# Order of the triangular solve of quarters two to four, and the PSUM bank of its combination

## The chip, the cores and the metric

The kernel runs on one core of a Trainium2 chip. The metric is the device time of one execution in microseconds, as the median of several runs of the same program. The core has a matrix engine (TensorE, PE in the profile; its weight loads are PEld), a vector engine (VectorE, DVE), an activation engine (ScalarE, ACT), a general engine (GpSimd, POOL) and a queue engine from which most DMAs are issued (SyncE, SP). Each engine works through its own list of instructions in the order in which the program has them, and waits on semaphores for the others.

## The reference

One inference step of a one-layer decoder trunk, over 512 prompt tokens and 8 x 8 sampled tokens (576 columns in the kernel). A shared projection feeds two groups of heads: a state-space group (SSD) and an RWKV-7 group, whose recurrence is

```python
def step(s, inp):
    r_t, w_t, k_t, v_t, kk_t, a_t = inp
    s_kk = jnp.einsum('bhvk,bhk->bhv', s, kk_t)
    s = (s * w_t[:, :, None, :] - s_kk[..., None] * (kk_t * a_t)[:, :, None, :]
         + v_t[..., None] * k_t[:, :, None, :])
    return s, jnp.einsum('bhvk,bhk->bhv', s, r_t)
```

with `kk = k*k_k / max(norm(k*k_k), 1e-12)` per head. Its readout goes through a norm per head, a bonus term and an output gate. Both groups then go through one output projection, a gated feed-forward layer, a per-layer embedding gate and a final norm. The step returns the two outputs and the new states.

## The kernel before

Activations lie transposed, 128 channels by 576 tokens. A projection is a sum of three matmuls per block, since weights and activations are split into a high and a low part (`whi`, `wlo`, `xhi`, `xlo`; L221 to L223 and L234). Weights come in blocks of 512 columns (`raw`, three buffers); ScalarE makes the high part (L93), GpSimd and VectorE in turn the low part (L206).

The RWKV heads are worked in four quarters (`Q[0]` to `Q[3]`; `s.q` is 0 for the first) of four heads each, two channel tiles `jj` with two heads `e`. In tokens there are nine groups `g` of 64: the sampled tokens and eight stretches of the prompt. A quarter goes through these steps:

- `fill_for` runs the six projections that the quarter needs; `fill` runs further projections of the list `todo` (the convolved columns `xbc`, the `z` gate) wherever the program puts them.
- `prep` makes the key norms and the decays. The sums of squared keys (L496) go to the PSUM bank `cb`, of which there is one (`cb_ps`); the square root of ScalarE (L93) that follows frees it. The transposes of the norms (`by_channel`, L523 and L526) use `cb` too.
- `start_states` (L734) multiplies the stored sampled states, loaded into `S0` (L723), also into `cb`. `S0` shares one buffer, tag `L`, with the matrix of the substitution and with the `S0` of `sampled` (L846 to L854).
- `gram` forms the products within a group (L613) and leaves a strictly triangular matrix per group and head in `Lst` (L623). `bonus` (L246, L598) and `decayed` (L650) follow.
- `inverse` is `solve` and then `combine`. `solve` needs the inverse of each 64 x 64 unit triangular matrix. It cuts the two diagonal blocks of 32 x 32 out through HBM (`Ld`, `L`), so that 72 blocks lie on 72 partitions, and inverts them on VectorE by substitution: 30 steps of two small instructions, each of which needs the one before (L674, L676). The results go through HBM back (`Td`, `Ad`), by SyncE's queue. `combine` loads them (`TT`, `AA`, L688 and L690), and makes the block below the diagonal with two small products: `Wp` (64 matmuls, L698), its eviction with a change of sign (L705 on VectorE, L93 on ScalarE), and `Xp` (64 matmuls, L712) with its eviction into `TT` (L719, L93). Both products took a bank of `cx_ps`, of which there are two.
- `chain` walks the nine groups in sequence (`core`, `prompt_state`, `outp`, `sampled`), with all its products in `cx` banks (L789, L797, L802, L812, L823, L849), and with small evictions on VectorE (L792, L805, L831) and ScalarE.
- `head_norm` is the norm per head of the quarter's result, with four products (L901) and the transposes of its norms (L523, L526) in `cx` banks.

The last quarter's `inverse`, `chain` and `head_norm` stand further down, among the start of the SSD part (`ssd`, a generator whose parts are called up by `SEQ`). There two kinds of fill are tied to a place: `issue_after(marks[...])` puts a `z` projection behind the last product (L901) of the third quarter's head norm (`("n", 2)`), the next one behind the last product L698 of the fourth quarter's combination (`("c", 3)`), and others behind steps of the fourth chain. The banks `r`, `y` and `d` of the SSD part open when the head norm of the last quarter is through.

The order on each engine is made when the program is built. A planner goes through a model of time; whenever an engine is free it gives it, out of the instructions that are ready in the model, the one that is first in the priority list, and it hands out buffers and banks on the way. The list is the order in which the code is written. `tc.high_priority()` puts the instructions of a block at the top of that list; the kernel has it at one place, the head norm of the last quarter. On the chip each engine then keeps that order.

Of the kernel before, what the change touches and what calls it, by code (L numbers as in the profile page):

```python
# [75 lines left out]
def hybrid_step(ctx, tc, A):  # L76
# [11 lines left out]
    def nm(s):  # L88
        uid[0] += 1
        return f"{s}_{uid[0]}"  # L90

    def act(out, in_, func=AF.Copy, scale=1.0, bias=0.0):
        return S.activation(out, in_, func, bias=bias, scale=scale)  # L93
# [16 lines left out]
    def bank(pool, tag, bufs):  # L110
        return pool.tile([P, 512], F32, tag=tag, name=nm(tag), bufs=bufs)
# [154 lines left out]
    def cx_ps():  # L266
        return bank(sq_, "cx", 2)
# [216 lines left out]
    def fill_at(s, i):  # L484
        fill(FP[s.q][i])
# [166 lines left out]
    def solve(s):  # L652

        q = s.q
        Ld = dp.tile([2, 2, 18, 32, 32], F32, tag=f"Ld{q}", name=f"Ld{q}")
        s.Td = dp.tile([2, 2, 18, 32, 32], F32, tag=f"Td{q}", name=f"Td{q}")
        s.Ad = dp.tile([2, 18, 32, 32], F32, tag=f"Ad{q}", name=f"Ad{q}")
        NB = 72
        for z in range(2):
            for e in range(2):  # L660
                r0 = e * 64 + z * 32
                nc.sync.dma_start(Ld[z, e].rearrange("g s t -> s g t"),
                                  s.Lst[r0:r0 + 32, :, :, z * 32:z * 32 + 32].rearrange("s g j t -> s (g j) t"))
        L = sp.tile([NB, 32, 32], F32, tag="L", name=nm("L"))
        nc.sync.dma_start(L[:], Ld[:].rearrange("z e g s t -> (z e g) s t"))
        Tt = s2.tile([NB, 32, 32], F32, tag="Tt", name=nm("Tt"))
        V.tensor_scalar(Tt[:], L[:], -1.0, None, ALU.mult)
        V.tensor_tensor(Tt[:].rearrange("p s t -> p (s t)")[:, 0:1024:33],
                        Tt[:].rearrange("p s t -> p (s t)")[:, 0:1024:33], ones[0:NB, 0:32], ALU.add)
        tmp = s2.tile([NB, 256], F32, tag="tmp", name=nm("tmp"))  # L670
        for jx in range(1, 31):
            n = 31 - jx
            o = tmp[:, 0:jx * n].rearrange("p (s t) -> p s t", s=jx)
            V.tensor_tensor(o, L[:, jx:jx + 1, jx + 1:32].to_broadcast([NB, jx, n]),  # L674
                            Tt[:, 0:jx, jx:jx + 1].to_broadcast([NB, jx, n]), ALU.mult)
            V.tensor_tensor(Tt[:, 0:jx, jx + 1:32], Tt[:, 0:jx, jx + 1:32], o, ALU.subtract)  # L676
        V.tensor_copy(L[0:36], Tt[0:36].rearrange("p s t -> p t s"))
        nc.sync.dma_start(s.Td[:].rearrange("z e g s t -> (z e g) s t"), Tt[:])
        nc.sync.dma_start(s.Ad[:].rearrange("e g s t -> (e g) s t"), L[0:36])

    def combine(s):

        TT = s.TT = inverses[s.q % 2]
        AA = s2.tile([P, 9, 2, 32], F32, tag="AA", name=nm("AA"))
        for e in range(2):
            for z in range(2):
                r0 = e * 64 + z * 32
                nc.sync.dma_start(TT[r0:r0 + 32, :, :, z * 32:z * 32 + 32].rearrange("s g j t -> s (g j) t"),  # L688
                                  s.Td[z, e].rearrange("g s t -> s g t"))
            nc.sync.dma_start(AA[e * 64:e * 64 + 32].rearrange("s g j t -> s (g j) t"),  # L690
                              s.Ad[e].rearrange("g s t -> s g t"))
        Wp = cx_ps()
        Wv = Wp[:].rearrange("p (g j t) -> p g j t", g=8, j=2)
        for g in range(1, 9):
            for jj in jj2:
                for e in range(2):
                    lo_, hi_ = e * 64, e * 64 + 32
                    marks["c", s.q] = T.matmul(Wv[hi_:hi_ + 32, g - 1, jj, :], s.Lst[lo_:lo_ + 32, g, jj, 32:64],  # L698
                                               AA[lo_:lo_ + 32, g, jj, :], start=True, stop=True)
        for e in range(2):  # L700
            hi_ = e * 64 + 32
            if e:
                act(AA[hi_:hi_ + 32, 1:9], Wv[hi_:hi_ + 32], scale=-1.0)
            else:
                V.tensor_scalar(AA[hi_:hi_ + 32, 1:9], Wv[hi_:hi_ + 32], -1.0, None, ALU.mult)  # L705
        Xp = cx_ps()
        Xv = Xp[:].rearrange("p (g j t) -> p g j t", g=8, j=2)
        for g in range(1, 9):
            for jj in jj2:
                for e in range(2):  # L710
                    lo_, hi_ = e * 64, e * 64 + 32
                    T.matmul(Xv[lo_:lo_ + 32, g - 1, jj, :], AA[hi_:hi_ + 32, g, jj, :],  # L712
                             TT[hi_:hi_ + 32, g, jj, 32:64], start=True, stop=True)
        for e in range(2):
            lo_ = e * 64
            if e:
                act(TT[lo_:lo_ + 32, 1:9, :, 32:64], Xv[lo_:lo_ + 32])
            else:
                V.tensor_copy(TT[lo_:lo_ + 32, 1:9, :, 32:64], Xv[lo_:lo_ + 32])  # L719
# [199 lines left out]
                YR.append(split(y, xp, ("xhi", "xlo"), [P, NT], lo_eng=V))  # L919

    def inverse(s):
        solve(s)
        fill_at(s, 7)
        combine(s)

    for s in Q:
        if s.q == 0:
            fill(2)
            gates(ugh)
        fill_for(s)  # L930
        prep(s)
        start_states(s)
        gram(s)
        bonus(s)
        decayed(s)
        if s.q < 3:
            inverse(s)
            chain(s)
            head_norm(s)
# [307 lines left out]
    steps = ssd()  # L1247
    next(steps)
    inverse(Q[3])
    s2_.close()  # L1250
    late.append(mix2.enter_context(tc.tile_pool(name="mf", bufs=1, reuse_waits="tile")))
# [421 lines left out]
```

## Time and profile before

| | us |
|---|---|
| median of three runs | 1342.29 |
| lowest and highest | 1341.25, 1345.83 |
| span of the profiled execution | 1349.0 |

The profile shows no other time of that execution than its span, from the first to the last instruction. All positions below are microseconds from its start. The profile is read with the engines' busy times, tables of windows, timelines of an engine (start, duration, engine, line, operation, what it writes and reads; in brackets the idle time before it and what ended it), groups of instructions by line, and lists of waits. A busy TensorE is not one at full speed: the granted clock is given beside it, 1.00 being full.

The chain of work that ended last is mostly TensorE's:

```profile
PE 63%; DVE 14%; ACT 4%; issue 4%; DMA 3%; POOL 3%; DVEq 0%; SPq 0%; ACTq 0%; POOLq 0%
```

The four quarters lie one after the other in the first half of the span: their substitutions start at 146.7, 276.2, 418.4 and 536.5 us. The chain of a quarter overlaps with the projections, the preparation and the substitution of the next one.

### The profile page before, as it was taken

Reading aid. Unit: us, or ns where it says so; the run is one execution under the profiler, and the core shown is the slowest. Engines: PE = TensorE matmul, PEld = TensorE weight load, DVE = VectorE, ACT = ScalarE, POOL = GpSimd, SP = SyncE. Lnnn points to the kernel's source line nnn. Section 1 sums busy time; section 2 is a strip of 40 time slices with the busy share of each in tenths; the row PEclk is TensorE's granted clock in tenths of the full one; section 3 lists DMA queues with packets and bytes.
Section 4 is the critical chain, followed back from the end, with each engine's and each line's share of the span. In section 5 each row is a group of like instructions: output and inputs, shape, how many; then the busy total and the mean of one; then the engine's idle time right before and its main releaser. Section 6 shows DMA issues by size and latency. Waiting matters only on the chain.

```text
span 1349.0 us, 26596 instructions
## 1 busy us (share of the span) xinstructions
PE 1246.8 (92%) x10525; PEld 1150.7 (85%) x10525; DVE 826.0 (61%) x1443; ACT 618.9 (46%) x1256; POOL 625.6 (46%) x597
## 2 busy tenths in 40 slices
PE   6897999999989978899999969989999999999997
PEld 6787897889868957788779859889999999999997
DVE  6648666887687785943466667886553135443454
ACT  6565436534654463343434364464442124433363
POOL 5425413642355154122456645565654336654642
PEclk9897799899979978889989989998999999999998
DMA  5322242234232412262454542222323222314322
GB/s 164 125 68 66 77 117 63 85 103 116 75 99 78 109 41 80 94 214 83 157 176 131 179 125 72 73 93 88 92 88 87 79 86 82 93 59 149 96 89 71
DMA packets 94461, 135.58 MB, mean 100 GB/s; under 512 B 34705, under 2 KB 39057, under 8 KB 94337
## 3 DMA queue, kind: packets, MB, share of 16 engines
q1 hardware_dynamic: 93760, 133.36, 32.4%
q8 instruction: 83, 1.36, 0.4%
q10 hardware_dynamic: 576, 0.52, 0.1%
q14 instruction: 42, 0.34, 0.1%
HBM read 106.10 MB, written 27.75 MB: 99 GB/s over the span
## 4 chain that ended last, share of the span: by engine, by line
PE 63%; DVE 14%; ACT 4%; issue 4%; DMA 3%; POOL 3%; DVEq 0%; SPq 0%; ACTq 0%; POOLq 0%
PE lin L234 21%; PE lin L1403 8%; PE lin L223 6%; PE lin L221 6%; PE lin L222 6%; DVE h L395 2%; PE lin L1508 1%; PE lin L1509 1%; PE lin L1510 1%; DVE tmp L674 1%; DVE wlo L206 1%; DVE Tt L676 1%; PE lin L613 1%; PE cx L797 1%; DVE suv L831 1%
## 5 line engine op out<-in xcount | busy, mean ns | idle before, releaser
L206 POOL TENSOR_TENSOR wlo<-raw,whi 128x512 fp32r<-128x512 f32 (+1 forms) x108 | 146.4, 1356 | 352.5 <-ACT whi L93 269.5
L93 ACT ACTIVATE whi<-raw 128x512 fp32r<-128x512 f32 (+1 forms) x232 | 143.3, 618 | 259.1 <-PE lin L234 126.4
L221 PE MATMUL lin<-xhi,whi 128*128 128x288 f32 (+1 forms) x784 | 243.3, 311 | 2.5 <-ACT whi L93 2.2
L223 PE MATMUL lin<-xhi,wlo 128*128 128x288 f32 (+1 forms) x784 | 241.5, 308 | 2.3 <-POOL wlo L206 2.3
L222 PE MATMUL lin<-xlo,whi 128*128 128x288 f32 (+1 forms) x784 | 241.5, 308 | 0.3 <-POOL xlo L194 0.3
L206 DVE TENSOR_TENSOR wlo<-raw,whi 128x512 fp32r<-128x512 f32 (+1 forms) x124 | 100.9, 814 | 103.2 <-PE lin L234 60.4
L221 PEld LDWEIGHTS lin<-xhi,whi 128*128 128x128 f32 (+1 forms) x784 | 151.0, 193 | 9.3 <-ACT whi L93 2.6
L223 PEld LDWEIGHTS lin<-xhi,wlo 128*128 128x128 f32 (+1 forms) x784 | 150.7, 192 | 6.2 <-POOL wlo L206 2.8
L222 PEld LDWEIGHTS lin<-xlo,whi 128*128 128x128 f32 (+1 forms) x784 | 150.8, 192 | 4.8 <-issue 1.2
L234 PE MATMUL lin<-xhi,whi 128*128 128x288 f32 x384 | 62.3, 297 | 3.2 <-ACT xhi L93 3.0
L234 PE MATMUL lin<-xlo,whi 128*128 128x288 f32 x384 | 60.8, 298 | 0.0
L234 PE MATMUL lin<-xhi,wlo 128*128 128x288 f32 x384 | 59.3, 297 | 0.0
L234 PEld LDWEIGHTS lin<-xhi,whi 128*128 128x128 f32 x384 | 54.6, 189 | 3.8 <-ACT xhi L93 1.7
L234 PEld LDWEIGHTS lin<-xlo,whi 128*128 128x128 f32 x384 | 54.8, 191 | 0.0
L234 PE MATMUL lin<-ah,wlo 128*128 128x288 f32 x352 | 54.7, 296 | 0.0
L234 PE MATMUL lin<-al,whi 128*128 128x288 f32 x352 | 54.7, 296 | 0.0
L234 PE MATMUL lin<-ah,whi 128*128 128x288 f32 x352 | 54.7, 296 | 0.0
L234 PEld LDWEIGHTS lin<-xhi,wlo 128*128 128x128 f32 x384 | 54.3, 191 | 0.0
L1403 PE MATMUL lin<-T,wh 128*128 128x288 f32 x320 | 50.1, 296 | 4.5 <-DVE T L194 2.8
L674 DVE TENSOR_TENSOR tmp<-L,Tt 72x30 f32<-72x30 f32 (+14 forms) x120 | 49.2, 410 | 3.2
L234 PEld LDWEIGHTS lin<-ah,whi 128*128 128x128 f32 x352 | 49.6, 189 | 0.0
L234 PEld LDWEIGHTS lin<-ah,wlo 128*128 128x128 f32 x352 | 49.6, 189 | 0.0
(425 smaller groups left out, 3197.8 us busy)
## 6 DMA issues: line engine op xcount, KB each, us to landing
raw<-wts SPq DMA_DIRECT2D x271, 256.0 KB, 2.6
S<-s_wkv SPq DMA_DIRECT2D x8, 512.0 KB, 5.1
hd<-s_ssm SPq DMA_DIRECT2D x8, 512.0 KB, 4.5
o_ssm_s<-hd SPq DMA_DIRECT2D x8, 512.0 KB, 2.9
xbc_d<-E SPq DMA_DIRECT2D x12, 288.0 KB, 2.1
x<-xT SPq DMA_DIRECT2D x8, 288.0 KB
gate_d<-g SPq DMA_DIRECT2D x8, 288.0 KB, 2.5
bv_d<-rw SPq DMA_DIRECT2D x8, 288.0 KB
```

What stands on the lines that cost most here:

```text
L93: return S.activation(out, in_, func, bias=bias, scale=scale)
L206: eng.tensor_tensor(lo[:, 0:n], raw[:, 0:n], hi[:, 0:n].bitcast(F32), ALU.subtract)
L221: T.matmul(ps[:, a:b], whi, xhi[:, a:b], start=first, stop=False)
L222: T.matmul(ps[:, a:b], whi, xlo[:, a:b], start=False, stop=False)
L223: T.matmul(ps[:, a:b], wlo, xhi[:, a:b], start=False, stop=last)
L234: T.matmul(ps[:, a:e], (hi, lo)[p][:, i * P:(i + 1) * P], xs[k + i][q][:, a:e], start=n == k + i == 0, stop=n == 2 and k + i == nk - 1, sk ...
L395: V.scalar_tensor_tensor(h[:], E[:, i:i + 600], w(i), h[:], ALU.mult, ALU.add)
L613: T.matmul(ps[:, c:c + 128].rearrange("p (a t) -> p a t", a=2), s.BK[jj][H[e], g].rearrange("p a t -> p (a t)"), s.G[H[e], g, jj, :, e], s ...
L674: V.tensor_tensor(o, L[:, jx:jx + 1, jx + 1:32].to_broadcast([NB, jx, n]), Tt[:, 0:jx, jx:jx + 1].to_broadcast([NB, jx, n]), ALU.mult)
L676: V.tensor_tensor(Tt[:, 0:jx, jx + 1:32], Tt[:, 0:jx, jx + 1:32], o, ALU.subtract)
L797: T.matmul(uw[H[e], jj, :], TT[H[e], g, jj, :], xs[H[e], jj, :], start=True, stop=True)
L1403: T.matmul(ps, (hi, lo)[p][:, k * P:(k + 1) * P], OPS[n][k][q], start=first and p == q == k == 0, stop=p == 1 and k == 3, skip_group_check ...
```

## The change

The substitution and the combination of quarters two to four are put at the top of the priority list, and the two products of their combination go to the bank `cb`. The first quarter stays as it was. No instruction is added, removed or altered otherwise.

```diff
@@ combine
-        Wp = cx_ps()
+        own = cb_ps if s.q else cx_ps
+        Wp = own()
...
-        Xp = cx_ps()
+        Xp = own()
@@ inverse
     def inverse(s):
-        solve(s)
+        with tc.high_priority() if s.q else nullcontext():
+            solve(s)
         fill_at(s, 7)
-        combine(s)
+        with tc.high_priority() if s.q else nullcontext():
+            combine(s)
```

`fill_at(s, 7)`, between the two, keeps its place; it is empty for quarters one to three and up to three projections for the fourth.

## Prediction

> **What bounds the kernel now.** I read the page's busy times first, then the table of windows, since one average hides stages with different limits. The rows give window and its length, PE busy with its count, PEld, DVE, ACT, POOL, the granted clock, DMA share and GB/s.
>
> ```profile
> span 1349.0 us, 26596 instructions
> PE 1246.8 (92%) x10525; PEld 1150.7 (85%) x10525; DVE 826.0 (61%) x1443; ACT 618.9 (46%) x1256; POOL 625.6 (46%) x597
> 285.00:330.00 45.00, 45.00 (x392) 41.72 (x392) 39.97 (x94) 16.66 (x41) 12.12 (x18) 0.99 0.38 103
> 330.00:370.00 40.00, 39.62 (x458) 36.11 (x457) 25.52 (x47) 26.23 (x54) 11.88 (x16) 1.00 0.29 93
> 370.00:412.00 42.00, 36.02 (x324) 28.50 (x323) 34.96 (x57) 24.39 (x58) 27.36 (x34) 0.76 0.27 84
> 515.00:530.00 15.00, 11.69 (x151) 10.01 (x148) 6.08 (x17) 5.14 (x16) 4.51 (x7) 0.77 0.12 37
> 557.00:576.00 19.00, 14.92 (x100) 11.48 (x101) 15.96 (x44) 5.13 (x12) 2.69 (x3) 0.64 0.23 69
> 583.00:594.00 11.00, 7.87 (x93) 7.23 (x92) 5.26 (x10) 5.48 (x10) 5.62 (x8) 0.69 0.34 112
> 690.00:830.00 140.00, 127.23 (x1144) 111.26 (x1143) 95.36 (x152) 65.50 (x147) 78.94 (x63) 0.94 0.43 137
> 830.00:1349.00 519.00, 501.95 (x3822) 498.22 (x3820) 263.13 (x345) 213.71 (x382) 274.02 (x205) 0.98 0.29 88
> ```
>
> The reader is to see that TensorE sets the time, and that the change can win only what TensorE loses: it alters no matmul. What a window loses I estimate as its length less PE busy times granted clock: 14.6 us in 370 to 412, 6.0 in 515 to 530, 9.5 in 557 to 576, 5.6 in 583 to 594, 20.4 in 690 to 830. In 285 to 370 TensorE is full (84.6 of 85 us). So work that starts sooner there gains nothing at that place. It gains if it then takes less of a stretch without projections to fill it.
>
> Next, the timelines of VectorE and of SyncE's queue around the substitution (L667 to L677) and its two DMA hops, for all four quarters (start, duration).
>
> ```profile
> 146.74 1.67 DVE L667 TENSOR_SCALAR Tt<-L 72x1024 f32<-72x1024 f32 x1
> 185.72 1.11 DVE L677 COPY L<-Tt 36x1024 f32<-36x1024 f32 x1
> 276.21 1.98 DVE L667 TENSOR_SCALAR Tt<-L 72x1024 f32<-72x1024 f32 x1 [3.78 <-DMA L<-Ld]
> 320.48 1.11 DVE L677 COPY L<-Tt 36x1024 f32<-36x1024 f32 x1
> 418.36 1.24 DVE L667 TENSOR_SCALAR Tt<-L 72x1024 f32<-72x1024 f32 x1 [5.03 <-DMA L<-Ld]
> 457.64 1.07 DVE L677 COPY L<-Tt 36x1024 f32<-36x1024 f32 x1
> 536.53 0.69 DVE L667 TENSOR_SCALAR Tt<-L 72x1024 f32<-72x1024 f32 x1 [3.40 <-DMA L<-Ld]
> 573.31 1.07 DVE L677 COPY L<-Tt 36x1024 f32<-36x1024 f32 x1
> L674 DVE TENSOR_TENSOR tmp<-L,Tt 72x30 f32<-72x30 f32 (+14 forms) x120 | 49.2, 410 | 3.2
> L676 DVE TENSOR_TENSOR Tt<-Tt,tmp 72x30 f32<-72x30 f32 (+14 forms) x120 | 45.2, 377 | 3.4
> ```
>
> From first to last the substitution takes 40.1, 45.4, 40.4 and 37.9 us (185.72 + 1.11 - 146.74, and so on), although its 60 small instructions are only (49.2 + 45.2) / 4 = 23.6 us. The rest is other VectorE work that slips in between two steps.
>
> Then the combination: the last load of AA on SyncE's queue, the landing time, and the first products (L698) in TensorE's timeline.
>
> ```profile
> 191.64 0.51 SPq L690 DMA_DIRECT2D AA<-Ad  x1
> 194.66 1.19 PE L698 MATMUL cx<-AA,Lst 32*32 32x32 f32 x62
> 326.51 1.49 SPq L690 DMA_DIRECT2D AA<-Ad  x1
> 341.92 1.20 PE L698 MATMUL cx<-AA,Lst 32*32 32x32 f32 x64
> 463.84 0.48 SPq L690 DMA_DIRECT2D AA<-Ad  x1
> 479.81 1.20 PE L698 MATMUL cx<-AA,Lst 32*32 32x32 f32 x64
> 578.84 0.50 SPq L690 DMA_DIRECT2D AA<-Ad  x1
> 588.43 1.92 PE L698 MATMUL cx<-AA,Lst 32*32 32x32 f32 x64
> DMA to landing us min/median/max: 2.2/2.2/2.2
> ```
>
> With 2.2 us to land, the data are there at 193.8, 328.7, 466.0 and 581.0. The products follow 0.8, 13.2, 13.8 and 7.4 us later. The first quarter has no older chain beside it; the other three wait until the head norm of the quarter before has finished with the two cx banks.
>
> **The change part by part.** Nothing is added or taken away; all costs are of order and of the bank.
>
> Substitution first in the list. The first quarter is the control: nothing older competes there, and still it takes 40.1 us, because a ready instruction of lower rank is let in while a step waits for the one before. So I take 45.4 - 40.1 = 5.3 us in the second quarter and 0 in the others. The ends are 0 and 23.6 plus about 3 us of start and copy, a gain of 11 to 19 us in each; the nearest row is the first quarter's 40.1. Its 7 DMAs (four Ld, L, Td, Ad) and the combination's 6 (four TT, two AA) move with it on SyncE's queue, past weight loads. The 6 loads hold the queue some 3 us at 0.3 to 1.5 us each, and three raw buffers hide that; without that cover TensorE would wait the 3 us. GpSimd gets nothing of either step. ScalarE gets two evictions a quarter, sooner.
>
> Combination without the head norm. Second quarter: 13.2 - 0.8 = 12.4 us sooner, all of it where TensorE is full, so 0 directly. The nine steps of its chain then leave 370 to 412 about one step sooner. Of the 14.6 us lost there I take 3; the ends are 0 and about 6, the time without PE busy.
>
> Third quarter. Here the one cb bank is itself taken, by the key sums of the fourth quarter, from the first row below to the last (PE, PE, then ScalarE's root that frees it):
>
> ```profile
> 460.02 0.28 PE L496 MATMUL cb<-blk,sqk 128*64 128x2 f32 x2
> 470.43 0.84 PE L496 MATMUL cb<-blk,sqk 128*64 128x2 f32 x22
> 472.13 0.18 ACT L93 ACTIVATE rn<-cb 128x20 f32<-128x20 f32 x1
> 505.84 2.87 POOL L585 TENSOR_TENSOR bk<-lo,lo 64x576 f32<-64x576 f32 x2
> 509.86 0.34 SPq L854 DMA_DIRECT2D o_wkv_s<-S  x1
> 514.82 0.33 SPq L723 DMA_DIRECT2D S<-s_wkv  x1
> 518.45 2.76 PE L734 MATMUL cb<-G,S 64*64 64x16 f32 x48 [2.34 <-DMA S<-s_wkv]
> 522.88 2.08 PE L613 MATMUL lin<-G,bk 64*128 64x128 f32 x16
> ```
>
> So it starts at 472.3 rather than 466.0, still 7.5 us before 479.81; if the bank is given to it first it starts at 466 and the key sums wait some 6 us instead. Behind a waiting product stand TensorE's gate matmuls and the key norms; VectorE's preparation waits for those. What the 7 us buy is in the last four rows: the sampled states of the third chain are stored at 509.86, which frees the buffer for the fourth quarter's states at 514.82, on which TensorE stands 2.34 us, with the Gram products (L613) queued behind. Sooner by 7, the states' products go into earlier gaps and L613 of 522.88 can follow at about 516.5. I take 6 us, the whole loss of 515 to 530. The ends are 0, if bk at 508.7 is late as well, and 13 with the bank free at once.
>
> Fourth quarter. The products come at 581.8 instead of 588.4. A projection of z is tied behind their last one, so TensorE would have work in this gap:
>
> ```profile
> 586.17 0.63 PE L769 MATMUL tr<-ident,bk 128*128 128x128 f32 x2 [3.00 <-ACT bkt L93]
> 562.58 1.22 PE L789 MATMUL cx<-suv,G 128*128 128x128 f32 x4 [2.85 <-DVE suv L831]
> ```
>
> The wait of 3.00 us is followed by matmuls at a lower granted clock (0.69 in 583 to 594, a loss of 5.6 us). I take 4; the ends are 0 and 5.6. [...]
>
> What it costs. In 557 to 576 no projection covers the third quarter's last chain steps, and its VectorE instructions (L792, L805, four of L831 in each of two steps, then four copies of the head norm: 16) now give way to a substitution step of about 0.4 us each: 0 to 6.4 us. I take 3, as the second row above shows such a wait costing 2.85 us at present. Products put at the head of TensorE's queue before AA has landed block it; the first quarter shows the price:
>
> ```profile
> PE cx L698 <- DMA AA<-Ad: 1.3, 1, 1.3
> ```
>
> I take 1.5 for the three quarters; the ends are 0 and 9.0, three times the 3.0 us from AA's last issue at 191.64 to the products at 194.66.
>
> The sum is -6 - 4 - 3 + 3 + 1.5 = -8.5 us. The span is 1349.0; the only other times shown are the three runs, whose median of 1342.29 is 6.7 us less, so I take the sum off the median: 1333.8 us.
>
> **The rivals.** *More than that.* The fourth chain starts some 13 us sooner (6 + 6.6); its head norm then frees the banks for the state-space part before 690 while projections are left to fill TensorE. Of the 20.4 us lost in 690 to 830, 10 would go: 1324. A substitution of 27 us in the third and fourth quarters would lead to about the same time, as each would bring the later chains 11 to 14 us forward. Against it: 600 to 690 is PE-bound, which stretches a chain step.
>
> *Nothing.* The preparation of the fourth quarter (bk at 508.7) sets the Gram products, not the states, or a promoted instruction has the place that it had before because its data decide: the 6 fall away, -2.5 is left, 1340.
>
> *Slower.* A promoted substitution holds back the chain of the quarter before where nothing covers it (557 to 576), and promoted products stand at the head of TensorE's queue before their data: 6.4 + 9.0 = 15.4 us, no gain in the third quarter, less the 4 and 3 of the other places, +8.4: 1350. It decides from the point at which the 16 VectorE instructions and the stops cost over 13 us together. For it speaks the wait of 2.85 us; against it that VectorE let the chain in between steps in all quarters. [...]
>
> **How the numbers follow.** The forecast has 0.40 (1329 to 1339), more than that 0.20, nothing 0.18, slower 0.22. Faster by over 0.3% (4 us, what a measurement can tell from no change) is 0.60, within it 0.18, slower 0.22. The range goes from 1319, where the larger gain is nearly whole, to 1352, with most of the slower case.
>
> **What would show it.** Right: L698 within 1 to 2 us of AA's landing in the second and fourth quarters, under 475 in the third; the stop of L734 on S gone; 515 to 530 shorter; the wait for bkt filled with z. Substitutions near 40 us. Wrong: substitutions of 27 us, a longer gap after the fill has run out before the last head norm, products waiting for AA, or later key sums with a later Gram stage.

## The result and the profile after

The changed kernel took 1353.49 us (median of 7 runs; 1345.83 for the kernel before beside it): a ratio of 1.0057, 95% interval 1.0033 to 1.0082. In a second comparison it was 1354.98 us, 1.0079 (1.0050 to 1.0107). So it is slower, by 8 to 12 us, where 8.5 us of gain had been forecast. The profile shown is of the second comparison, since the first profiled execution was a disturbed one. Lines behind L691 of the old program stand one further down here (the first products are L699, the second L713), those behind `inverse` three; experiments that add lines shift them by a few more.

The page of the changed kernel, its span, busy times and the chain that ended last:

```profile
span 1353.4 us, 26585 instructions
PE 1246.6 (92%) x10525; PEld 1149.7 (85%) x10525; DVE 826.7 (61%) x1443; ACT 617.6 (46%) x1256; POOL 623.5 (46%) x597
PE 55%; DVE 21%; DMA 5%; issue 4%; ACT 4%; POOL 2%; SPq 0%; DVEq 0%; ACTq 0%; POOLq 0%
```

TensorE is as busy as before (1246.6 against 1246.8 us). VectorE's share of the chain has risen from 14 to 21%, TensorE's has fallen from 63 to 55%: TensorE stands more often behind work on VectorE. The table of windows, with the cuts of the prediction and four more:

```profile
285.00:330.00 45.00, 42.40 (x337) 39.45 (x338) 36.19 (x87) 14.93 (x37) 10.16 (x15) 0.94 0.37 106
330.00:370.00 40.00, 39.21 (x454) 35.27 (x454) 23.90 (x41) 22.64 (x50) 13.63 (x14) 0.94 0.19 62
370.00:412.00 42.00, 35.89 (x329) 30.14 (x329) 37.44 (x61) 25.71 (x56) 21.09 (x31) 0.81 0.30 94
425.00:490.00 65.00, 61.72 (x636) 56.28 (x634) 49.80 (x122) 28.12 (x64) 14.24 (x15) 0.95 0.31 91
490.00:545.00 55.00, 46.20 (x419) 34.98 (x421) 38.84 (x85) 28.47 (x66) 26.30 (x32) 0.78 0.20 59
515.00:530.00 15.00, 14.31 (x172) 12.53 (x172) 9.73 (x24) 7.11 (x21) 6.14 (x9) 0.65 0.02 7
545.00:610.00 65.00, 59.97 (x592) 52.98 (x588) 49.30 (x114) 27.29 (x56) 13.11 (x17) 0.89 0.49 155
557.00:576.00 19.00, 14.38 (x112) 11.29 (x113) 16.77 (x43) 4.82 (x12) 3.53 (x4) 0.75 0.27 89
583.00:594.00 11.00, 11.00 (x195) 10.55 (x193) 6.93 (x12) 7.12 (x14) 3.25 (x3) 1.00 0.69 189
610.00:690.00 80.00, 73.42 (x627) 59.49 (x628) 28.79 (x71) 33.65 (x83) 32.69 (x29) 0.94 0.41 131
690.00:830.00 140.00, 127.18 (x1100) 110.46 (x1099) 92.70 (x152) 62.34 (x145) 77.75 (x63) 0.91 0.42 137
```

The extra windows for the kernel before:

```profile
425.00:490.00 65.00, 58.41 (x625) 52.74 (x626) 54.03 (x123) 33.96 (x73) 14.03 (x17) 0.95 0.32 93
490.00:545.00 55.00, 48.48 (x467) 37.89 (x468) 36.02 (x83) 22.36 (x59) 26.32 (x29) 0.87 0.23 63
545.00:610.00 65.00, 57.78 (x556) 50.98 (x555) 43.59 (x104) 24.92 (x52) 11.29 (x15) 0.84 0.48 155
610.00:690.00 80.00, 76.03 (x658) 61.01 (x657) 34.03 (x78) 35.94 (x86) 36.38 (x32) 0.97 0.41 132
```

Length less busy time times clock gives the loss, as in the prediction. It has risen from 0.8 to 8.3 us in 285 to 370, where TensorE had been full, and from 12.8 to 19.0 us in 490 to 545. It has fallen from 14.6 to 12.9 us in 370 to 412, from 9.5 to 6.4 in 425 to 490 and from 16.5 to 11.6 in 545 to 610, where 583 to 594 has gone from 5.6 to 0. Behind that it has risen again, from 6.3 to 11.0 us in 610 to 690 and from 20.4 to 24.3 in 690 to 830. So the change gains in some stretches and loses more in others: in the second quarter, in the third, and behind 610. The windows are cut at the same times in both traces, though the stages have moved by some us, and the trace of the kernel before is itself one of its longer executions (1349.0); a difference of 1 or 2 us in a row says little.

The second quarter first, in timelines of the changed kernel (substitution on VectorE, last load of AA on SyncE's queue, then TensorE):

```profile
274.00 1.98 DVE L667 TENSOR_SCALAR Tt<-L 72x1024 f32<-72x1024 f32 x1 [3.79 <-DMA L<-Ld]
318.13 1.11 DVE L677 COPY L<-Tt 36x1024 f32<-36x1024 f32 x1
323.76 0.50 SPq L690 DMA_DIRECT2D AA<-Ad  x1
324.95 0.31 PE L699 MATMUL cb<-AA,Lst 32*32 32x32 f32 x2 [2.60 <-DMA AA<-Ad]
328.00 0.44 PE L223 MATMUL lin<-xhi,wlo 128*128 128x288 f32 x1
328.24 0.44 PE L221 MATMUL lin<-xhi,whi 128*128 128x288 f32 x1
331.01 1.19 PE L699 MATMUL cb<-AA,Lst 32*32 32x32 f32 x62
333.46 0.29 PE L221 MATMUL lin<-xhi,whi 128*128 128x288 f32 x1
333.59 0.29 PE L222 MATMUL lin<-xlo,whi 128*128 128x288 f32 x1
```

The substitution takes 45.2 us (318.13 + 1.11 - 274.00), as before. The combination does start 17 us earlier (324.95 for 341.92), but two of its products stand at the head of TensorE's queue and hold it for 2.60 us; the projections behind follow each other every 0.24 us (328.00 to 328.24) instead of every 0.13 (333.46 to 333.59). From 318 to 345 us TensorE is busy for 24.40 us at a granted clock of 0.87, which by the formula above is a loss of 5.8 us, the stop and 3.2 us more; in the kernel before it is 0.2 there (26.85 us at 1.00). The list of waits has both stops of this kind:

```profile
PE cb L699 <- DMA AA<-Ad: 4.6, 2, 2.6
```

What this gains and what it displaces shows in TensorE's timelines, the first and the third row of the kernel before, the second and the fourth of the changed one: the first product of the second quarter's chain, which the combination is for, and the first decay projection of the third quarter's preparation.

```profile
348.62 0.71 PE L789 MATMUL cx<-suv,G 128*128 128x128 f32 x4
346.69 0.61 PE L790 MATMUL cx<-suv,G 128*128 128x128 f32 x4
350.62 0.29 PE L221 MATMUL lin<-ulh,whi 128*128 128x288 f32 x1
357.13 0.29 PE L221 MATMUL lin<-ulh,whi 128*128 128x288 f32 x1
```

The chain starts only 1.9 us sooner (its first product that reads TT comes 3.1 us sooner, at 348.4 us for 351.5), although the combination's last eviction ends at 339.2 us (338.64 + 0.59) where it ended at 350.5; the first quarter's head norm, ahead of the chain in the cx banks, has its last transpose at 343.29 us, for 339.12 before. The decay projection comes 6.5 us later.

The third quarter, same kernel: the first products, ScalarE's eviction of the second products, then the fourth quarter's key sums on TensorE, the root of them, the products of its stored states and GpSimd's last work on `bk`.

```profile
473.14 0.24 PE L699 MATMUL cb<-AA,Lst 32*32 32x32 f32 x2 [2.02 <-DMA AA<-Ad]
486.30 0.59 ACT L93 ACTIVATE TT<-cb 32x512 f32<-32x512 f32 x1
487.74 1.33 PE L496 MATMUL cb<-blk,sqk 128*64 128x2 f32 x40
491.25 0.19 ACT L93 ACTIVATE rn<-cb 128x20 f32<-128x20 f32 x1
517.56 1.80 PE L735 MATMUL cb<-G,S 64*64 64x16 f32 x48
519.29 2.86 POOL L585 TENSOR_TENSOR bk<-lo,lo 64x576 f32<-64x576 f32 x2 [8.50 <-DVE lo L581]
```

The combination holds the one cb bank from 473.1 to 486.9 us. The key sums of the fourth quarter, which ended at 471.3 before, get it at 487.7, and with them the key norms and the whole preparation come later: `bk` is complete at 522.2 us (519.29 + 2.86) instead of 508.7.

### The profile page after: what moved, and what is told of

Same layout as the page of the kernel before. It is cut to its first block, busy times and chain, and to the rows that moved or that the text cites. A ratio compares the mean times of both kernels' runs of the same rounds, so it can differ in the third digit from the quotient of the medians.

```text
span 1363.6 us, 26585 instructions
## 1 busy us (share of the span) xinstructions
PE 1259.7 (92%) x10525; PEld 1162.8 (85%) x10525; DVE 830.2 (61%) x1443; ACT 618.1 (45%) x1256; POOL 624.1 (46%) x597
## 4 chain that ended last, share of the span: by engine, by line
PE 56%; DVE 18%; DMA 6%; issue 5%; ACT 4%; POOL 2%; SPq 0%; DVEq 0%; POOLq 0%; ACTq 0%
PE lin L234 21%; PE lin L1406 8%; PE lin L223 5%; PE lin L221 5%; PE lin L222 4%; DVE Tt L676 2%; DVE tmp L674 2%; DVE h L395 1%; DVE suv L832 1%; DVE wlo L206 1%; DMA raw<-wts 1%; PE lin L613 1%; DMA L<-Ld 1%; ACT G L93 1%; PE cx L790 1%
## 5 line engine op out<-in xcount | busy, mean ns | idle before, releaser
L223 PE MATMUL lin<-xhi,wlo 128*128 128x288 f32 (+1 forms) x784 | 245.6, 314 | 2.5 <-POOL wlo L206 2.2
L221 PEld LDWEIGHTS lin<-xhi,whi 128*128 128x128 f32 (+1 forms) x784 | 153.0, 195 | 11.6 <-ACT whi L93 2.8
L234 PEld LDWEIGHTS lin<-al,whi 128*128 128x128 f32 x352 | 49.6, 189 | 0.0
```

The lines of the kernel that those rows point to most:

```text
L221: T.matmul(ps[:, a:b], whi, xhi[:, a:b], start=first, stop=False)
L223: T.matmul(ps[:, a:b], wlo, xhi[:, a:b], start=False, stop=last)
L234: T.matmul(ps[:, a:e], (hi, lo)[p][:, i * P:(i + 1) * P], xs[k + i][q][:, a:e], start=n == k + i == 0, stop=n == 2 and k + i == nk - 1, sk ...
```

## The experiments

Two theories stood at first. **A**: the bank does it, through products that enter TensorE's order before their operand has landed. **B**: the priority does it, as the promoted substitution holds back the older chain. Later came **C**: what costs is that the next quarter's preparation comes late, and the combination's own place matters little; and **D**: any other order of this program is slower by about as much.

The table gives for each kernel the ratio of its time to that of the kernel before in the same comparison, with the 95% interval, and puts the traces side by side, in us from the start of the span: when VectorE's eviction into TT of the second quarter starts (L719 of the old program), the last Gram mask (L623) of the third and of the fourth quarter, and the last product of the fourth head norm (L901). *prio_only* has the order of the kernel before (8 of 8789 entries of TensorE's list stand elsewhere), and its trace differs from that of the kernel before by 1.6, 5.4 and 6.1 us in the last three columns; smaller differences there mean nothing. So the fourth quarter's mask of the changed kernel is clearly later than that of prio_only (10.5 us), but not than that of the kernel before (5.1); its `bk`, 13.4 us later than in the kernel before, is clearly late.

| kernel | ratio (interval) | TT, second | Gram, third | Gram, fourth | head norm |
|---|---|---|---|---|---|
| before | 1 | 348.7 | 411.4 | 529.5 | 681.1 |
| prio_only | 1.0000 (0.9978, 1.0022) | 347.2 | 409.8 | 524.1 | 675.1 |
| after_again, the change | 1.0079 (1.0050, 1.0107) | 337.9 | 418.6 | 534.6 | 688.0 |
| bank_only | 1.0076 (1.0050, 1.0102) | 342.8 | 420.7 | 533.0 | 686.2 |
| after_tied | 1.0141 (1.0115, 1.0167) | 344.8 | 418.4 | 536.2 | 699.5 |
| after_tied_n | 1.0070 (1.0045, 1.0095) | 341.1 | 421.0 | 538.0 | 690.5 |
| bank_q1 | 1.0092 (1.0064, 1.0120) | 337.8 | 419.2 | 536.0 | 692.1 |
| bank_q2 | 1.0105 (1.0074, 1.0137) | 347.5 | 410.2 | 535.8 | 688.3 |
| bank_q3 | 1.0062 (1.0037, 1.0087) | 348.1 | 410.7 | 528.1 | 683.4 |
| prep_late2 | 1.0104 (1.0080, 1.0128) | 350.6 | 423.9 | 541.8 | 692.9 |
| keys_late3 | 1.0148 (1.0111, 1.0184) | 346.9 | 409.5 | 538.1 | 692.9 |
| after_prep | 1.0291 (1.0260, 1.0323) | 343.1 | 426.9 | 554.0 | 717.4 |
| before_prep | 1.0301 (1.0271, 1.0330) | 357.9 | 419.9 | 544.2 | 713.1 |
| kf3 | 1.0071 (1.0044, 1.0098) | 351.8 | 414.5 | 539.0 | 692.0 |
| tied_q1 | 1.0083 (1.0051, 1.0116) | 346.9 | 419.0 | 537.0 | 688.4 |
| tied_q1_keep | 1.0028 (1.0006, 1.0051) | 344.1 | 408.3 | 528.6 | 683.9 |

### Bank or priority

prio_only leaves the banks as before; bank_only leaves the priorities as before.

```diff
 prio_only
-        own = cb_ps if s.q else cx_ps
+        own = cx_ps
 bank_only
-        with tc.high_priority() if s.q else nullcontext():
-            solve(s)
+        solve(s)
         fill_at(s, 7)
-        with tc.high_priority() if s.q else nullcontext():
-            combine(s)
+        combine(s)
```

> Both blocks at the top of the list, the combination in the cx banks as before. A: 0.997 to 1.003, products at the places they had before, no wait for AA in quarters two to four. B: 1.004 to 1.008.

> The bank cb for the combination of quarters two to four, no priority. A: 1.004 to 1.008, L699 waiting 4 to 6 us for AA. B: 0.997 to 1.003.

> The changed kernel itself, to have it beside the others on one chip. Theory A (bank): with its own bank the combination's first products (L699) are put into TensorE's order before AA has landed; TensorE stops there and runs at a lower granted clock behind it. Theory B (priority): the substitution at the top of the list holds back the VectorE evictions of the chain of the quarter before. Both: 1.004 to 1.008 of the kernel before. A adds: L699 waits for AA about 5 us in quarters two to four together, with matmuls spaced 0.24 rather than 0.13 us behind the first two stops.

The bank alone gives the whole loss, the priority nothing. With the cx banks a block at the top of the list has the place that it had before (8 of 8789 entries), presumably because its instructions were already given out as soon as their data were there. With the bank cb the priority does move things (the second quarter's first products are at 324.95 us in the changed kernel, at 330.42 in bank_only), but the time is the same. B falls.

### The stops on AA

Both kernels are the changed one with the first products tied behind work of the quarter before: behind the last transpose of its head norm, or behind the last of its products L901.

```diff
 after_tied
+with tc.issue_after(marks["h", s.q - 1].ins) if s.q else nullcontext():
     for g in range(1, 9):
...
 after_tied_n
+with tc.issue_after(marks["n", s.q - 1].ins) if s.q else nullcontext():
```

> The changed kernel, with the first product of quarters two to four tied on TensorE behind the last transpose of the head norm of the quarter before (about 85, 23 and 0 projection matmuls later than in the changed kernel, that is 11, 3 and 0 us). A: no wait for AA over 0.5 us, and the loss gone: 0.997 to 1.003. B: 1.004 to 1.008, as the priorities are all there.

> The changed kernel, with the first products tied behind the head norm's last centring product (L902) of the quarter before. On TensorE this turns only one thing round: in the second quarter the four L902 go ahead of the two products instead of behind them. A: they fill 1.2 to 2.3 us of the stop of 2.9, and the clock stays up: 2 to 5 us less than the changed kernel, so 1.001 to 1.006 of the kernel before. B: as the changed kernel within 0.1%.

after_tied has no wait of cb products for AA left, and is slower still; in after_tied_n waits of 4.3 us remain and nothing is gained. The Gram mask of the third quarter stays late, at 418.4 and 421.0 us. A names a real loss, but not the one that decides. Why after_tied is 0.6% worse than the changed kernel was not followed further.

### One quarter at a time

`own = cb_ps if s.q == k else cx_ps` for k = 1, 2, 3, the rest as in the changed kernel.

> The changed kernel, but only the combination of the second quarter in cb, the others in cx. A: this is where the stop was longest (2.91 us, and some 6 us of matmuls at half speed behind it, together about 6 us): 1.003 to 1.006. B: 1.004 to 1.008, as all priorities are there.

> Only the combination of the third quarter in cb. A: a stop of about 1.9 us and some 6 us of slow matmuls, together about 5 us, against which a chain that starts up to 5 us sooner counts: 0.999 to 1.004. B: 1.004 to 1.008.

> Only the combination of the fourth quarter in cb. A: its products come some 18 projection matmuls sooner than in the changed kernel, so a stop of 1 to 2.5 us, against the wait for bkt of 3.0 us that projections of z can now fill: 0.997 to 1.002. B: 1.004 to 1.008.

Each alone costs about as much as the three together, so the costs don't add up; why they don't was not followed. The table shows where: bank_q1 moves the third quarter's Gram mask by 8 to 9 us, bank_q2 leaves that and moves the fourth quarter's, though its combination is 14 us sooner (VectorE's eviction into TT at 472.1 us, 485.6 in prio_only). Every kernel that was late at the third quarter's mask is late at the fourth's too. In bank_q2 the bank is seen at work (ScalarE, then TensorE):

```profile
474.84 0.59 ACT L93 ACTIVATE TT<-cb 32x512 f32<-32x512 f32 x1
476.40 0.98 PE L496 MATMUL cb<-blk,sqk 128*64 128x2 f32 x28
```

bank_q3 has no later quarter to delay. Its eviction into TT is 4.9 us sooner than in prio_only (587.8 against 592.7), but the chain starts at 590.9 instead of 590.3 us, so that came to nothing, and a new stop stands further down (TensorE, the split that it waited for, the loads of that split's data):

```profile
670.67 0.40 PE L221 MATMUL lin<-xhi,whi 128*128 128x288 f32 x1 [3.41 <-ACT xhi L93]
669.94 0.68 ACT L93 ACTIVATE xhi<-yl 128x576 fp32r<-128x576 f32 x1 [3.75 <-DMA yl<-yr_d]
664.26 2.25 SPq L1270 DMA_DIRECT2D yl<-yr_d  x2
```

And two windows of it:

```profile
660.00:670.00 10.00, 6.76 (x73) 6.18 (x71) 4.63 (x12) 3.39 (x10) 3.23 (x3) 1.00 0.69 205
670.00:680.00 10.00, 8.93 (x57) 7.36 (x58) 2.16 (x7) 4.92 (x11) 5.54 (x4) 0.66 0.46 138
```

The fill of this stretch has presumably been used up sooner, so that TensorE reaches a product whose operand is just being loaded; the stop costs 3.41 us, and the lower clock behind it some 3 us more (the second window loses 10 - 8.93 x 0.66 = 4.1 us, the same window of prio_only, at 8.77 us and a clock of 1.00, 1.2). That this is the whole of bank_q3's loss was not tested.

### The preparation late, or first

prep_late2 and keys_late3 are the kernel before with one tie each, which delays preparation and leaves the combination in cx. before_prep and after_prep put the preparation of quarters two to four at the top of the list.

```diff
 prep_late2   (lora, the decay and gate factors)
+with tc.issue_after(marks[1, 0].ins) if q == 2 and jj == 0 else nullcontext():
     mm3(ps, wl[0][:, c], wl[1][:, c], UL[0], UL[1], True, True)
 keys_late3
+with tc.issue_after(marks["c", 2].ins) if q == 3 else nullcontext():
     token_sums(st, jj, sq)
 before_prep, after_prep
+with tc.high_priority() if s.q else nullcontext():
     prep(s)
```

> The kernel before, with one tie: the two small products that open the preparation of the third quarter's first channel tile (written by the decay and gate factors, 349.1 and 355.2 us in the trace of the kernel before) are queued behind the second step of the second quarter's chain (355.5 us). The combination keeps its banks, its place and its time. Theory C (what costs is that the next quarter's preparation comes late; the combination's own place matters little): the last Gram mask of the third quarter comes at 417 to 421 instead of 410 to 411.5 us, and the ratio to the kernel before is 1.004 to 1.010. Theory A (stops of TensorE on the combination's operand, and the lower clock behind them): no combination product moves, so the ratio is within 0.002 of 1. Theory D (any other order of this program is slower by about as much, wherever it differs): 1.004 to 1.010 too, but without the later Gram mask.

> The kernel before, with one tie: the sums of squared keys of the fourth quarter (458 to 471 us in the trace of the kernel before) are queued behind the first products of the third quarter's combination (478 to 480 us), which stay in their cx bank. So the key sums come as late as they do where the combination has the bank cb, but the combination is not sooner. Theory C: the last Gram mask of the fourth quarter comes at 533 to 537 instead of 524 to 529.6 us, and the ratio to the kernel before is 1.004 to 1.010, like that of the kernel with cb in the third quarter alone (1.0105). If instead the combination in cb was what cost there (its own wait, its evictions), the ratio is within 0.002 of 1. Theory D: 1.004 to 1.010 without the later Gram mask.

> The changed kernel with the preparation of quarters two to four at the top of the priority list too. Theory C: with the preparation no longer behind the earlier chain, the last Gram masks of the third and fourth quarters come by 412 and 528 us (418.7 and 534.7 in the changed kernel), and the ratio to the kernel before falls from 1.008 to 0.996 to 1.002. Theory A: the products of the combination still wait for their operand, and the ratio stays at 1.005 to 1.010. Theory D: it stays above 1.004, whatever the masks do.

> The kernel before with the preparation of quarters two to four at the top of the priority list; substitution, combination and banks as before. Theory C: the Gram masks come as early as before or earlier, and the ratio is 0.992 to 1.000. Theory A says nothing of it beyond 1.000, since no combination product gets ahead of its operand. Theory D: 1.004 to 1.010, because the order is another one.

A late preparation alone, with no combination moved, costs 1.0 and 1.5%, more than the change does, and moves the same masks, though further (the third quarter's by 12.5 us and the fourth's by 8.7; the change moves them by 7.2 and 5.1): C holds in this half. The other half failed. With the preparation first, the masks come later still (420 to 427 and 544 to 554 us) and the kernels are 3% slower, before and after alike. The second quarter's chain is held back (its first product is at 357.77 us in before_prep, at 348.62 in the kernel before); why the masks are late as well was not followed. So C's forecast failed here, and as the masks came later and not sooner, these kernels don't show what an earlier preparation would bring. The priority of the whole preparation is no means to put it right.

### An earlier combination with the preparation kept

tied_q1 has cb in the second quarter alone, tied as in after_tied, which leaves its first products about where they were (339.62 us, 340.41 in prio_only). tied_q1_keep is the same, with one projection of the fill put behind the decay projection; there the first products come at 336.88 us. kf3 has cb in the third quarter alone, and the key sums of the fourth quarter are written ahead of that combination, so that they get the bank first, as the prediction had it.

```diff
 tied_q1_keep
-        fill_at(s, 0)
+        if q != 2: fill_at(s, 0)
...
             ip = lora(0, jj, hw[:, j:j + 1])
+            if q == 2 and jj == 0:
+                with tc.issue_after(marks["l"].ins): fill_at(s, 0)
 kf3
         fill_at(s, 7)
+        if s.q == 2:
+            fill_for(Q[3])
+            Q[3].st = keys(Q[3])
         ...
         combine(s)
```

In kf3 the chain and the head norm of the third quarter stand at the top of the list too, since the six projections are now written ahead of them; the same program with cx keeps the order of the kernel before but for some ten entries of TensorE's list.

> Third quarter alone, as the prediction had put it: its combination goes to cb, but the fourth quarter's key sums are written ahead of it in the program and get the bank first. Up to the key sums the order of TensorE is that of the kernel before; the first products come behind the last key sum instead of behind the head norm's last transpose. Theory C: the last Gram mask of the fourth quarter stays at 524 to 530 us, and as the preparation did not move, the ratio to the kernel before is 0.997 to 1.003; it is 1.0105 where the bank goes to the combination first. The prediction's term (6 us of 1343) would be 0.9955, with the first products at 472 to 474 us instead of 478 to 480. Theory D (any other order here is slower): 1.004 to 1.010.

> Second quarter alone: its combination goes to cb, its first products tied behind the last transpose of the first quarter's head norm, so that they do not wait for their operand; the other quarters keep cx. Theory C: the first decay projection of the next preparation is parted by 24 matmuls of another projection, as in the kernel with all three tied, so the third quarter's last Gram mask comes at 417 to 420 us instead of 410 to 411.5, and the ratio is 1.004 to 1.010. Theory A: no stop, so 1.000 within 0.002.

> The same as the kernel before it in this list, with the projection that parted the decay projection put behind it, where it stands in the kernel before the change. Theory C: the third quarter's Gram mask is back at 409 to 412 us although the combination is still earlier, and the ratio is 0.997 to 1.003. Theory D: 1.004 to 1.010 as without this.

Where tied_q1's preparation falls behind that of prio_only, one projection has come in between. First the first decay projection (`ulh`, `ull`, two halves of three matmuls) in prio_only, first and last, and then the same in tied_q1:

```profile
349.11 0.29 PE L221 MATMUL lin<-ulh,whi 128*128 128x288 f32 x1
349.77 0.29 PE L223 MATMUL lin<-ulh,wlo 128*128 128x288 f32 x1
```

```profile
349.64 0.41 PE L221 MATMUL lin<-ulh,whi 128*128 128x288 f32 x1
349.88 0.29 PE L222 MATMUL lin<-ull,whi 128*128 128x288 f32 x1
356.32 0.38 PE L223 MATMUL lin<-ulh,wlo 128*128 128x288 f32 x1
```

In tied_q1 the third matmul comes 6.2 us behind the second, with another projection between; the tanh, the decays and the Gram products follow, and the mask is at 419.0 us. With that projection put behind, the mask is at 408.3 us, and the ratio falls from 1.0083 to 1.0028 (the intervals touch at 1.0051). So in tied_q1 most of the loss goes with the late preparation. It is not a pure test: the planner orders what follows anew, the first decay projection is at 341.13 us, 8.0 sooner than in prio_only, and the kernel before with the same projection moved was not run. And the earlier combination brought nothing: the chain's first product (L789 of the old program) comes at 340.15 instead of 347.11 us in prio_only, the last products of that quarter's head norm come 2.3 us sooner (463.54 against 465.87), and the kernel is no faster than before. How much a combination another 6 us sooner, as in the changed kernel, would bring with the preparation kept was not tried.

kf3 answers the same for the third quarter (ScalarE and TensorE; L704 and L523 with `rx` are the first products and the transposes of the key norms):

```profile
473.56 0.84 PE L496 MATMUL cb<-blk,sqk 128*64 128x2 f32 x22
475.79 1.20 PE L704 MATMUL cb<-AA,Lst 32*32 32x32 f32 x64
485.98 0.59 ACT L93 ACTIVATE TT<-cb 32x512 f32<-32x512 f32 x1
486.63 0.74 PE L523 MATMUL cb<-ident,rx 128*128 128x128 f32 x4 [1.57 <-ACT TT L93]
```

This trace is 4.7 us later than that of prio_only up to here (the key sums end at 473.56 + 0.84 = 474.4 against 469.7 us). The key sums keep their place, and the first products come right behind them. But now the transposes of the key norms find the bank taken: they stand until ScalarE has evicted the combination, at 486.63 instead of 477.67 us, 4.3 later beyond the shift. `bk` is complete 4.2 us later beyond the shift (515.95 against 507.07), the mask, at 539.0 us, 10.2 (6.4 by the trace of the kernel before, where the key sums ended at 471.3), and the ratio is 1.0071. What adds the rest between `bk` and the mask was not followed. C's own figure for it (0.997 to 1.003) was a miss, since it counted the key sums as the only user of the bank.

D is not settled. tied_q1_keep came out better than D had said (1.004 to 1.010), but every kernel here whose order differs from the old one in more than a few entries was slower, tied_q1_keep too (1.0006 at the least). That the old order is hard to better wherever it is touched remains a rival for a part of each loss.

## Why the prediction was wrong

- **What bounds the kernel** was read rightly: TensorE's losses, not its work, set the time. But every term looked at what an earlier combination would *release*, and none priced what it *displaces*. In all kernels that are slower by 0.7% or more the Gram stage of the third or the fourth quarter comes later. Even the release was small: in the changed kernel the chains of the three quarters start at 346.69, 481.46 and 594.04 us, for 348.62, 484.97 and 595.78 before.
- **Third quarter, -6 us: the step that failed.** The prediction saw that the bank is taken by key sums, chose the case in which they go first, and named the key norms behind a waiting product without a price. The planner gave the bank to the combination; the end of the key sums moved from 471.3 to 489.1 us (487.74 + 1.33). The bank in this quarter alone (bank_q2) costs 1.05%. With the key sums first, the key norms wait instead, and kf3 costs 0.7%. The stop of L734 on S did go (the states' products start at 517.56 without a wait, on a buffer freed in time), as forecast, and bought nothing, because `bk` was now the late one (522.2 us for 508.7). A late `bk` was in the text as the end at 0, without the change making it later; the true end lay beyond it.
- **Second quarter, -3 us.** The window 370 to 412 lost 1.7 us less, of the size that was forecast, but hardly by the way forecast: the chain started 1.9 us sooner, not a step. It was bought with 7.5 us more loss in 285 to 370, which the prediction held to be free since TensorE is full there; 5.6 of them are the stop of 2.60 us and the lower clock behind it (318 to 345). A full engine was not free either: what entered its queue pushed something back, the decay projection, by 6.5 us. The bank in this quarter alone (bank_q1) costs 0.9%.
- **Substitution first, 5.3 us in the second quarter.** It takes 45.2 us as before, and the priority alone gives 1.0000. The term that the promoted substitution would hold back the chain (+3) is 0 for the same reason. This part of the rival *Slower* fell, too.
- **Products before their operand, +1.5.** Right in kind, too small: 2.60 and 2.02 us, 4.6 in all, and 3.2 more by the lower clock behind the first. But the kernels in which the ties removed the stops are no better (tied_q1 has 1.0083, bank_q1, with the stop, 1.0092), so the stops alone don't explain the result.
- **Fourth quarter, -4 us.** The window 583 to 594 lost 0 instead of 5.6 us, and the wait for bkt is gone: right at its place. Against it, 610 to 830 lost 8.6 us more; presumably the z projection that filled the gap was missing there. bank_q3 alone is 0.6% slower, with a new stop of 3.41 us. Which of the terms missed this cost stays open.
- **The rivals.** *Slower* (1350) had nearly the time, by luck: its 16 VectorE instructions and its stops at 9.0 us are not what was measured. The sign by which the text would have known it was there as its last: later key sums with a later Gram stage.

## What to carry to other kernels

A full engine may hide less than it seems (7.5 us more loss in 285 to 370 here): when a step moves forward in its queue, name the step that moves back, and follow that one to its next consumer. Before a step is given a bank that "is free", list all users of that bank until the step's last eviction, not only the one that holds it at the moment (in kf3 the transposes of the key norms, a user that had not been counted, came 4.3 us later). And where a planner builds the order, look at the order first: here a priority changed next to nothing (1.0000 in prio_only), and a bank a great deal (1.0076 in bank_only).

## What the runs showed of the hardware that was not expected

The clock: after a stop of 2.60 us TensorE's projections were issued every 0.24 instead of every 0.13 us for some 3 us (changed kernel; granted clock 0.87 in 318 to 345 us, 1.00 in the kernel before), and after one of 3.41 us the granted clock was 0.66 in 670 to 680 us (bank_q3; 1.00 in prio_only). The prediction had it from a stop of 3.00 us; the first of these is shorter. Whether the length of a stop decides was not shown: in the kernel before the clock was 0.50 in 484 to 490 us, and the longest stop in the 12 us ahead of that was 1.13 us (L712, at 483.42).

The bank: in kf3, where one bank serves two stages, TensorE stood 1.57 us until ScalarE's eviction of the first was through (485.98 + 0.59 us; the transposes of the second start at 486.63), besides the order that puts the waiting matmuls behind.

The spread: one program, the kernel before, took from 1337.6 to 1351.6 us in these comparisons, and single profiles of nearly the same order lie 11 us apart (1349.0 in the kernel before, 1337.9 in prio_only).
